# A two-layer diffusion backbone on one core: mixer inputs settled by thirds, the mixer's root on VectorE, the first convolution tap on ScalarE, two score units placed earlier

## The chip, the core and the metric

The kernel runs on one core of one Trainium2 chip. The metric is the device time of one execution in microseconds (us); the time before is the median of three runs. Names used for the engines: PE is the matmul engine (TensorE), DVE is VectorE, ACT is ScalarE, POOL is GpSimd, and SP is SyncE, which issues nearly all transfers.

## What is computed

Two layers of a hybrid backbone over 384 tokens of width 1024: 128 context tokens and 256 latent tokens. Each layer is a half-step feed-forward block, a token mixer, and a second half-step feed-forward block, each behind an RMS norm that is scaled and shifted by a conditioning vector ("ada"). Cut to the mixer:

```python
def _layer(x, cvec, lp, mixer):
    ...
    h = _rmsnorm(x, lp["norm_g"][1]) * (1.0 + sc2) + sh2
    y, ctx = mixer(h)
    x = x + g2 * y
    ...

def _mixer_latent(h, lp, na_kc, na_vc, gq_kc, gq_vc):
    u_hy, na_q, na_k, na_v, gq_q, gq_k, gq_v = _project(h, lp)   # one input projection, q and k RMS-normed
    y_hy = _hyena(u_hy, lp)                                      # short 3-tap convolution, then a long one by FFT
    y_na = _neighbourhood_attention(na_q, na_k, na_v, na_kc, na_vc, lp["na_rpb"])
    y_gq = _window_attention(_axial_rope(gq_q), _axial_rope(gq_k), gq_v, gq_kc, gq_vc, lp["gqa_sink"])
    return _merge(y_hy, y_na, y_gq, lp), ()                      # one output projection

def _short_conv(u, w, b):
    n = u.shape[1]
    up = jnp.pad(u, ((0, 0), (1, 1), (0, 0)))
    return up[:, 0:n] * w[0] + up[:, 1:n + 1] * w[1] + up[:, 2:n + 2] * w[2] + b
```

The long convolution's filter is itself the output of a small sine network, taken to the frequency domain. The context tokens go through the same mixer with dense attention; their keys and values are outputs too (`o_nk`, `o_nv`, `o_gk`, `o_gv`).

## The kernel before

All products with the large weights are done in fp32 as three passes: a weight block comes in as `raw` by a transfer from SP, ACT rounds it to `whi` (L141), DVE subtracts to get `wlo` (L142), the activations are split the same way into `mh` and `ml`, and `mm3` (L303 to L305) issues the three matmuls, 0.18 us apart. A generator of blocks (`get`, `ahead`) keeps the split three blocks ahead of PE. Besides, a slow job runs on DVE through the whole program: the conditioning products (`ada_tick`, L205), a set number of halves of a block for each weight block.

Nothing reorders the instructions: each engine takes them in the order in which the Python code emits them, and waits at the first that isn't ready. The order of the mixer is written out by hand. The main sequence is: the Hyena projection (`hy`, two groups of three output tiles, four weight blocks each), then the projections `pq`, `pk`, `pkv`, `pg`, `vN` (three PSUM tiles `pj` each; PE rows of all of them read `pj<-whi` and so on), then the attention "slots", then the output projection `po`. Between weight blocks `work(budget)` takes steps of the background generators in a list (`bg`): `conv_bg` (the short convolution), `filt` (the filter network, its taps, and its transform `kf`, which ACT copies to `K`), `na_post`, `gk_post`, `gq_post` (norm, scale and rotation of what a projection gave), and `fft`. Each `yield` gives the step's weight against the budget, so one yield less moves everything behind it in the list earlier.

The mixer's own norm is deferred: the projection runs on the unnormed `x` times the ada scale, and the factor is applied to the result. `stats1` (L338) sums the squares by PE (`pss`) and works 1/sqrt by DVE and, from the third operation on, POOL (`rsqrt`, L307: two operations, then 13 that depend on one another). `spread_r` (L345) puts the three values of each token on the diagonals of `dg`, `stats2` (L351) spreads them over the partitions by one product (`pr`) into `R`. `explicit` multiplies the inputs by `R` and ada's scale and shift for the later projections, `settle` splits them into `mh` and `ml`, and `deferred` (L359) applies `R` to a finished tile of the Hyena projection (`hyt`). `HYS = (1, 0)` says after which blocks this happens: the root behind the second block of the first group, `R` behind the first of the second group.

An attention unit is a head pair and a query tile, `hs[0]` to `hs[11]`. A `slot` (L973) does, for successive units, the scores on PE (`sc`), the largest value on DVE (`nm`), the division of an earlier unit's weights (`pr`, L874), their transposition on PE (`pp`), the products with the values (`py`), and the exponentials on ACT (`pr`, L914 and L920). `un_bias` asks for a unit's masks (`nab`). Before, all slots stand behind `vN`.

Buffers matter here. PSUM tiles come from four buffers for each of two tags, "a" and "b"; `kf`, `sc`, `gk`, `pp` and the small products all share "b". Most SBUF tiles of the mixer (`tt`) come from one pool of tag "t", handed out in turn, so that a new tile takes the oldest buffer and waits for everything that still reads it. In the rows of the trace, `pr` names several tiles: the product of `stats2` (L354), and the softmax weights, which the code calls `pr0` and, for the context keys of a unit's first query tile, `pr2`.

`gk_post` ends with the output copies `o_gk` and `o_gv`, issued by POOL (L1053, L1054). POOL's queue holds in this order: the root for gq's norm (13 operations), then `o_gk`, `o_gv`, then `o_nv`.

Of the kernel before, what the change touches and what calls it, by code (L numbers as in the profile page):

```python
# [11 lines left out]
AF = mybir.ActivationFunctionType  # L12
ALU = mybir.AluOpType
# [3 lines left out]
KD = D // P  # L17
# [14 lines left out]
MIXRATE = ((0.75, 0, 0, 0), (0.45, 0, 0, 0))  # L32
# [3 lines left out]
GA = 2  # L36
DLATE = 8
WLATE = False
HYS = (1, 0)
STAT = ((0, 2), (2, 4))  # L40
HPLAN = ({4: (0, 1), 5: (2, 3), 6: (4, 5), 7: (6, 7)}, {4: (0, 1), 5: (2, 3), 6: (4, 5), 7: (6, 7)})
LATE0 = 1
# [36 lines left out]
def _build(ctx, tc, nc, A):  # L79
# [10 lines left out]
    V, S, T = nc.vector, nc.scalar, nc.tensor  # L90

    def tt(name, dt=F32, w=388):
        return tp.tile([P, w], dt, tag="t", name=name)

    def ps(name, tag="b"):
        return psp.tile([P, 512], F32, tag=tag, name=name)

    def sm(name, w=64, dt=F32):
        t = smp.tile([P, 64], dt, tag="s", name=name)
        return t[:, :w]  # L100
# [23 lines left out]
    def small(name, i, n=1):  # L124
        o = SM[name][0] + i
        return sml[:, o:o + n]
# [13 lines left out]
    def split(src, hi, lo):  # L140
        S.activation(hi, src, AF.Copy)  # L141
        V.tensor_tensor(lo, src, hi.bitcast(F32), op=ALU.subtract)  # L142
# [86 lines left out]
    def ada_next():  # L229
        if not adaq:  # L230
            return
        (l, p, j), w = adaq[0]
        ada_half(l, p, j, side_v[0], w)
        side_v[0] ^= 1
        if side_v[0] == 0:
            done.add((l, p, j))
            if p % 3 == 1:
                ada_scale(l, p // 3, j, j + 1)
            adaq.pop(0)
            ada_load()  # L240
# [8 lines left out]
    def ada_tick(rate):  # L249
        credit[0] += 2 * rate  # L250
        while credit[0] >= 1.0:
            credit[0] -= 1.0
            ada_next()
# [84 lines left out]
    def stats1(G=nc.gpsimd):  # L338
        acc = accq
        pss = ps("pss")  # L340
        for t in range(3):
            T.matmul(pss[:, t:t + 1], acc[:, t * P:(t + 1) * P], ones[:, 0:1], start=True, stop=True)
        return rsqrt(pss[:, 0:3], 3, 1.0 / D, G)

    def spread_r(r):  # L345
        dg = tt("dg", w=NT)
        for t in range(3):
            V.tensor_scalar(dg[:, t * P:(t + 1) * P], ident, r[:, t:t + 1], None, op0=ALU.mult)
        return dg

    def stats2(r, dg=None):  # L351
        dg = spread_r(r) if dg is None else dg
        pr = ps("pr")
        T.matmul(pr[:, :NT], ones, dg, start=True, stop=True)  # L354
        R = tt("R", w=NT)
        S.activation(R, pr[:, :NT], AF.Copy)
        return R

    def deferred(pss, R, name):  # L359
        b = sm("bc", 2)  # L360
        V.tensor_copy(b, pss[:, NT:386])
        t = tt(name, w=NT)
        V.tensor_tensor(t, pss[:, :NT], R, op=ALU.mult)  # L363
        return t, b

    def explicit(l, i, R, ks):
        hs = [tt("h", w=NT) for _ in ks]
        for h, k in zip(hs, ks):
            V.tensor_tensor(h, xT[k], R, op=ALU.mult)
        for h, k in zip(hs, ks):  # L370
            for v, a, b in SEG:
                g, sh = gsc[l][:, i, k, v:v + 1], mod[l][:, 3 * i, k, v:v + 1]
                if k in HDVE:
                    V.tensor_scalar(h[:, a:b], h[:, a:b], g, sh, op0=ALU.mult, op1=ALU.add)
                else:
                    S.activation(h[:, a:b], h[:, a:b], AF.Identity, scale=g, bias=sh)
        return list(zip(hs, ks))

    def settle(hk):
        for h, k in hk:  # L380
            split(h, mh[k][:, :NT], ml[k][:, :NT])
# [155 lines left out]
    def mixer(l, after):  # L537
# [11 lines left out]
        def drain(g):  # L549
            while g in bg:  # L550
                try:
                    next(g)
                except StopIteration:
                    bg.remove(g)
# [91 lines left out]
        uc, tm = {}, {}  # L646

        def conv(n):
            up = tt("up")
            for c in (0, 129, 386):  # L650
                V.memset(up[:, c:c + 1], 0.0)
            for v, a, e in SEG:
                S.activation(
                    up[:, 1 + v + a:1 + v + e], tm[n][0][:, a:e], AF.Identity, bias=tm[n][1][:, v:v + 1]
                )
            o = tt(f"uc{n}")
            w3 = [small("conv_w", (l * 3 + q) * 6 + n) for q in range(3)]
            V.tensor_scalar(o[:, 1:386], up[:, 0:385], w3[0], small("conv_b", l * 6 + n), op0=ALU.mult, op1=ALU.add)
            for q in (1, 2):
                V.scalar_tensor_tensor(o[:, 1:386], up[:, q:q + 385], w3[q], o[:, 1:386], op0=ALU.mult, op1=ALU.add)  # L660
            uc[n] = o

        pu = {}
        hk = []
        for grp in range(2):
            for i in range(3):
                pu[grp * 3 + i] = ps(f"hy{i}", "ab"[grp])
            for kb in range(4):
                hi, lo = get()
                for kk, i in order2(2, 3, kb == 3):  # L670
                    k = kb * 2 + kk
                    s = slice(kk * 384 + i * P, kk * 384 + (i + 1) * P)
                    mm3(pu[grp * 3 + i][:, :386], (hi[:, s], lo[:, s]), (mh[k], ml[k]), k == 0, k == KD - 1)
                ahead()
                if (grp, kb) == (0, HYS[0]):
                    rs = stats1()
                if (grp, kb) == (0, 3):
                    dg = spread_r(rs)
                ada_tick(MIXRATE[l][grp])
                if (grp, kb) == (1, HYS[1]):  # L680
                    R = stats2(rs, dg)
                if grp == 1 and kb > HYS[1]:
                    n = KD // (3 - HYS[1]) if HYS[1] != 0 else 3
                    c = kb - HYS[1] - 1
                    hn = explicit(l, 1, R, range(n * c, min(n * c + n, KD)))
                    settle(hk)
                    hk = hn
                    tm[c] = deferred(pu[c], R, "hyt")

        Y = [[None, None] for _ in range(KD)]  # L690

# [2 lines left out]
            split(src, *Y[t])  # L694

        def conv_bg():
            settle(hk)
            yield 1.0
            for n in [n for n in range(6) if n not in tm]:
                tm[n] = deferred(pu[n], R, "hyt")  # L700
                yield 0.55
            for n in range(6):
                conv(n)
                yield 1.2
            for c in range(2):
                V.tensor_tensor(uc[c][:, 1:386], uc[c][:, 1:386], uc[2 + c][:, 1:386], op=ALU.mult)
            yield 0.95

        def project(n, kper, mid):
            pt = [ps(f"pj{t}", "a") for t in range(3)]  # L710
            for kb in range(KD // kper):
                hi, lo = get()
                for kk, t in order2(kper, 3, kb == KD // kper - 1):
                    k = kb * kper + kk
                    s = slice(kk * n, (kk + 1) * n)
                    c = slice(t * P, (t + 1) * P)
                    mm3(pt[t][:, :n], (mh[k][:, c], ml[k][:, c]), (hi[:, s], lo[:, s]), k == 0, k == KD - 1)
                ahead()
                ada_tick(MIXRATE[l][2])
                if kb < KD // kper - 1:  # L720
                    mid(kb)
            out = []
            for t in range(3):
                o = tt("pj", w=NT)
                S.activation(o[:, :n], pt[t][:, :n], AF.Copy)
                out.append(o)
            mid(KD // kper - 1)
            return out
# [108 lines left out]
        def whole(kb):  # L837
            work(BUD[0])
# [8 lines left out]
        q_it = add(na_post(pq, False), True)  # L847
        loads2()
        pk = project(384, 2, whole)
        k_it = add(na_post(pk, True), True)  # L850
# [122 lines left out]
        def slot():  # L973
            s = slot_n[0]
            slot_n[0] += 1
            if s == 0:
                un_bias(hs[0])
                un_bias(hs[1])
            if s + 2 < len(hs):
                un_bias(hs[s + 2])  # L980
            if s < len(hs):
                un_score(hs[s])
            if 0 <= s - 1 < len(hs):
                un_norm(hs[s - 1])
            if 0 <= s - 2 < len(hs):
                un_turn(hs[s - 2])
            if 0 <= s - 3 < len(hs) and hs[s - 3].qi:
                un_pv(hs[s - 3])
            if s < len(hs):
                un_exp(hs[s])  # L990
            work(BUD[2])
# [70 lines left out]
        gk_it = add(gk_post(pkv), True)  # L1062
        pg = project(384, 2, whole)
        gq_it = add(gq_post(pg))
        vN = project(384, 2, whole)
        nc.gpsimd.dma_start(out=A["o_nv"][l], in_=vN[0])
        drain(q_it)
        drain(k_it)
        drain(conv_it)
        drain(filt_it)  # L1070
        fft_it = add(fft())
# [303 lines left out]
```

## Time and profile before

| | us |
|---|---|
| median of three runs | 1540.18 (1538.29 to 1541.30) |
| the profiled execution | 1536.43 |
| its span, first to last instruction | 1534.6 |
| PE busy | 1499.8 (98%) |
| DVE busy | 1144.1 (75%) |
| ACT busy | 649.9 (42%) |
| POOL busy | 70.8 (5%) |

The two mixers lie at about 313 to 478 us and 1062 to 1228 us of the span. A row of a timeline gives start, duration, engine, line and operation; what stands in brackets is the time for which that engine had been idle, and the instruction whose end released it. Matmul durations overlap, so the distance of two starts tells the pace.

### The profile page before, as it was taken

The numbers are of one execution on the slowest core, as the hardware profiler recorded it, in microseconds if no ns is written. First come the engines' busy times: TensorE is split into PE (matmuls) and PEld (weight loads), VectorE is DVE, ScalarE is ACT, GpSimd is POOL, SyncE is SP. The second block draws the span as 40 slices with busy tenths as digits, with TensorE's granted clock in tenths as the row PEclk, the third lists the DMA queues.
The fourth block names the chain that finished last, engine by engine and source line by source line (L and its number), as shares of the span: only waits on it lengthen the run. The fifth ranks groups of instructions, "written<-read, shape, count | busy, mean of one in ns | idle before, by whom it ended". The sixth has DMA issues, their size and how long they took to land. (4 is left out here: it accounts for less than half of the span.)

```text
span 1534.6 us, 23110 instructions
## 1 busy us (share of the span) xinstructions
PE 1499.8 (98%) x8636; PEld 1440.9 (94%) x8636; DVE 1144.1 (75%) x2198; ACT 649.9 (42%) x1191; POOL 70.8 (5%) x181
## 2 busy tenths in 40 slices
PE   6999999999989999999999999999999999999999
PEld 4999999999769999999999999999996799999998
DVE  4489998879787689877858888887897767644444
ACT  3533333346566443333334333333556645433221
POOL 0000000013300000000000000001131000000000
PEclk9999999999999999999999999999999999999999
DMA  9656666564412446655544565556543133344342
GB/s 318 236 183 232 238 226 237 209 195 150 128 42 80 154 162 222 220 196 199 181 152 144 195 238 204 208 210 219 165 124 101 34 124 127 118 158 136 121 153 73
DMA packets 89733, 261.27 MB, mean 170 GB/s; under 512 B 10097, under 2 KB 27796, under 8 KB 89492
## 3 DMA queue, kind: packets, MB, share of 16 engines
q1 hardware_dynamic: 89236, 258.74, 49.2%
q8 instruction: 68, 1.11, 0.3%
q0 software_dynamic: 384, 1.05, 0.2%
q14 instruction: 45, 0.37, 0.1%
HBM read 257.13 MB, written 2.62 MB: 169 GB/s over the span
## 5 line engine op out<-in xcount | busy, mean ns | idle before, releaser
L142 DVE TENSOR_TENSOR wlo<-raw,whi 128x1024 fp32r<-128x1024 f32 (+2 forms) x352 | 394.7, 1125 | 132.3 <-ACT whi L141 131.9
L303 PE MATMUL up<-mh,whi 128*128 128x384 f32 (+1 forms) x1408 | 478.9, 340 | 4.5 <-ACT mh L141 4.2
L305 PE MATMUL up<-mh,wlo 128*128 128x384 f32 (+1 forms) x1408 | 476.9, 339 | 1.3 <-DVE wlo L142 1.2
L304 PE MATMUL up<-ml,whi 128*128 128x384 f32 (+1 forms) x1408 | 477.3, 339 | 0.7 <-DVE ml L142 0.7
L141 ACT ACTIVATE whi<-raw 128x1024 fp32r<-128x1024 f32 (+2 forms) x352 | 339.0, 974 | 270.6 <-PE dn L304 119.5
L205 DVE CUSTOM_DVE_ANT_0 junk<-adaw,cb,sml 128x1024 bf16<-128x1024 f32 x256 | 332.5, 1299 | 2.1
L303 PEld LDWEIGHTS up<-mh,whi 128*128 128x128 f32 x1408 | 265.5, 189 | 7.5 <-ACT mh L141 5.9
L305 PEld LDWEIGHTS up<-mh,wlo 128*128 128x128 f32 x1408 | 265.8, 189 | 2.6 <-DVE wlo L142 2.6
L304 PEld LDWEIGHTS up<-ml,whi 128*128 128x128 f32 x1408 | 265.4, 188 | 2.4 <-DVE ml L142 2.0
L305 PE MATMUL dn<-gh,wlo 128*128 128x384 f32 x704 | 237.2, 337 | 0.0
L304 PE MATMUL dn<-gl,whi 128*128 128x384 f32 x704 | 237.1, 337 | 0.0
L303 PE MATMUL dn<-gh,whi 128*128 128x384 f32 x704 | 236.9, 336 | 0.0
L141 ACT ACTIVATE gh<-t 128x384 fp32r<-128x384 f32 x76 | 39.9, 525 | 294.6 <-DVE t L486 286.4
L303 PEld LDWEIGHTS dn<-gh,whi 128*128 128x128 f32 x704 | 132.2, 188 | 0.0
L304 PEld LDWEIGHTS dn<-gl,whi 128*128 128x128 f32 x704 | 132.1, 188 | 0.0
L305 PEld LDWEIGHTS dn<-gh,wlo 128*128 128x128 f32 x704 | 132.1, 188 | 0.0
L303 PE MATMUL pj<-whi,mh 128*128 128x384 f32 (+1 forms) x240 | 80.1, 334 | 0.8 <-DVE hyt L363 0.8
L305 PE MATMUL pj<-whi,ml 128*128 128x384 f32 (+1 forms) x240 | 78.2, 326 | 0.0
L304 PE MATMUL pj<-wlo,mh 128*128 128x384 f32 (+1 forms) x240 | 78.2, 326 | 0.0
L486 DVE TENSOR_TENSOR t<-up,t 128x384 f32<-128x384 f32 x72 | 39.8, 553 | 50.3 <-PE up L305 50.2
L142 DVE TENSOR_TENSOR gl<-t,gh 128x384 fp32r<-128x384 f32 x76 | 42.4, 558 | 45.0 <-ACT gh L141 45.0
L313 POOL TENSOR_SCALAR rs_r<-rs_r 128x18 int32<-128x18 int32 (+2 forms) x13 | 8.3, 640 | 1172.0 <-DVE rs_r L312 1149.3
(221 smaller groups left out, 1573.2 us busy)
## 6 DMA issues: line engine op xcount, KB each, us to landing
raw<-w SPq DMA_DIRECT2D x184, 512.0 KB, 4.4
adaw<-ada SPq DMA_DIRECT2D x128, 512.0 KB, 3.5
raw<-w SPq DMA_DIRECT2D x64, 448.0 KB, 4.7
raw<-win SPq DMA_DIRECT2D x48, 384.0 KB, 4.0
raw<-w13a SPq DMA_DIRECT2D x32, 384.0 KB, 3.2
adw<-ada SPq DMA_DIRECT2D x32, 192.0 KB, 4.5
raw<-woa SPq DMA_DIRECT2D x16, 384.0 KB, 3.1
nab<-nab SPq DMA_DIRECT2D x24, 192.0 KB, 2.4
```

What stands on the lines that cost most here:

```text
L141: S.activation(hi, src, AF.Copy)
L142: V.tensor_tensor(lo, src, hi.bitcast(F32), op=ALU.subtract)
L205: V.tensor_tensor_reduce(out=junk, in0=w, in1=cb[:, v, :], scale=scale, scalar=small("ada_b", (l * NADA + p) * KD + j), op0=ALU.mult, op1= ...
L303: T.matmul(out, ah, bh, start=start, stop=False)
L304: T.matmul(out, ah, bl, start=False, stop=False)
L305: T.matmul(out, al, bh, start=False, stop=stop)
L313: G.tensor_scalar(r.bitcast(I32), r.bitcast(I32), -1.0, float(0x5F3759DF), op0=ALU.mult, op1=ALU.add)
L486: V.tensor_tensor(t1, PQ[1][:, :NT], t1, op=ALU.mult)
```

## The change

It has three parts. (A) In the Hyena projection the root is worked wholly by DVE behind the second block and spread on `dg` at once; `R` comes behind the third block, and the inputs are scaled by thirds (three, three, two of the eight) behind blocks four to six, settled, with one `hyt` each, behind blocks six to eight. `HYS` goes, the `ada_tick` of the projection takes the first group's rate for three blocks, and `conv_bg` begins without a settle of its own, one `yield` less. (B) The first of the three convolution taps, with the bias, is an activation on ACT instead of a `tensor_scalar` on DVE. (C) Slots 0 and 1 are run inside the `vN` projection, behind its second and third weight block; the background steps of q and k are drained ahead of the first of them. The number of slots doesn't change, so what was in slot 2 comes first behind `vN`.

```diff
--- before.py
+++ after.py
@@ -36,7 +36,6 @@
 GA = 2
 DLATE = 8
 WLATE = False
-HYS = (1, 0)
 STAT = ((0, 2), (2, 4))
 HPLAN = ({4: (0, 1), 5: (2, 3), 6: (4, 5), 7: (6, 7)}, {4: (0, 1), 5: (2, 3), 6: (4, 5), 7: (6, 7)})
 LATE0 = 1
@@ -655,7 +654,9 @@
                 )
             o = tt(f"uc{n}")
             w3 = [small("conv_w", (l * 3 + q) * 6 + n) for q in range(3)]
-            V.tensor_scalar(o[:, 1:386], up[:, 0:385], w3[0], small("conv_b", l * 6 + n), op0=ALU.mult, op1=ALU.add)
+            S.activation(
+                o[:, 1:386], up[:, 0:385], AF.Identity, scale=w3[0], bias=small("conv_b", l * 6 + n)
+            )
             for q in (1, 2):
                 V.scalar_tensor_tensor(o[:, 1:386], up[:, q:q + 385], w3[q], o[:, 1:386], op0=ALU.mult, op1=ALU.add)
             uc[n] = o
@@ -672,20 +673,18 @@
                     s = slice(kk * 384 + i * P, kk * 384 + (i + 1) * P)
                     mm3(pu[grp * 3 + i][:, :386], (hi[:, s], lo[:, s]), (mh[k], ml[k]), k == 0, k == KD - 1)
                 ahead()
-                if (grp, kb) == (0, HYS[0]):
-                    rs = stats1()
-                if (grp, kb) == (0, 3):
-                    dg = spread_r(rs)
-                ada_tick(MIXRATE[l][grp])
-                if (grp, kb) == (1, HYS[1]):
-                    R = stats2(rs, dg)
-                if grp == 1 and kb > HYS[1]:
-                    n = KD // (3 - HYS[1]) if HYS[1] != 0 else 3
-                    c = kb - HYS[1] - 1
-                    hn = explicit(l, 1, R, range(n * c, min(n * c + n, KD)))
-                    settle(hk)
-                    hk = hn
-                    tm[c] = deferred(pu[c], R, "hyt")
+                s = grp * 4 + kb
+                if s == 1:
+                    dg = spread_r(stats1(V))
+                elif s == 2:
+                    R = stats2(None, dg)
+                if s < 3:
+                    ada_tick(MIXRATE[l][0])
+                elif s < 6:
+                    hk += explicit(l, 1, R, range(3 * (s - 3), min(3 * (s - 2), KD)))
+                if s > 4:
+                    settle(hk[3 * (s - 5):3 * (s - 4)])
+                    tm[s - 5] = deferred(pu[s - 5], R, "hyt")
 
         Y = [[None, None] for _ in range(KD)]
 
@@ -694,8 +693,6 @@
             split(src, *Y[t])
 
         def conv_bg():
-            settle(hk)
-            yield 1.0
             for n in [n for n in range(6) if n not in tm]:
                 tm[n] = deferred(pu[n], R, "hyt")
                 yield 0.55
@@ -1062,10 +1059,17 @@
         gk_it = add(gk_post(pkv), True)
         pg = project(384, 2, whole)
         gq_it = add(gq_post(pg))
-        vN = project(384, 2, whole)
+
+        def first_units(kb):
+            whole(kb)
+            if kb == 1:
+                drain(q_it)
+                drain(k_it)
+            if kb in (1, 2):
+                slot()
+
+        vN = project(384, 2, first_units)
         nc.gpsimd.dma_start(out=A["o_nv"][l], in_=vN[0])
-        drain(q_it)
-        drain(k_it)
         drain(conv_it)
         drain(filt_it)
         fft_it = add(fft())
```

How the instructions move is shown at two places. In the program's line numbers of the change, lines are one to three lower than in the kernel before. `[waits X]` says on which engine's or transfer queue's count the instruction waits.

On ACT, in the first layer, from the squares of gq's norm (`q`) on; before:

```order
L738 ACTIVATE q_4028<-pj 128x384 [waits PE_49,Activation_49]
L738 ACTIVATE q_4031<-pj 128x384 [waits DVE_49,Activation_49]
L738 ACTIVATE q_4034<-pj 128x384 [waits DVE_49,Activation_49]
L141 ACTIVATE whi<-raw 128x768 [waits DMAHW0_49,PE_49]
L623 ACTIVATE K_3296<-kf,sml 128x256 [waits DMASW0_49,PE_49]
L623 ACTIVATE K_3299<-kf,sml 128x256 [waits DVE_49,PE_49]
L623 ACTIVATE K_3302<-kf,sml 1x256 [waits DVE_49,PE_49]
L141 ACTIVATE whi<-raw 128x768 [waits DMAHW1_49]
L1057 ACTIVATE kTG_3608<-gk 128x128 [waits PE_49]
L1058 ACTIVATE kTG<-gk 128x256
L623 ACTIVATE K_3297<-kf,sml 128x256 [waits PE_49]
```

and with the change:

```order
L622 ACTIVATE K_3299<-kf,sml 128x256 [waits DVE_49,PE_49]
L622 ACTIVATE K_3302<-kf,sml 128x256 [waits DVE_49,PE_49]
L622 ACTIVATE K_3305<-kf,sml 1x256 [waits DVE_49,PE_49]
L735 ACTIVATE q_4038<-pj 128x384 [waits Activation_49]
L735 ACTIVATE q_4041<-pj 128x384 [waits Activation_49]
L735 ACTIVATE q_4044<-pj 128x384 [waits Activation_49]
L140 ACTIVATE whi<-raw 128x768 [waits DMAHW0_49]
L622 ACTIVATE K_3300<-kf,sml 128x256 [waits DMASW0_49,PE_49]
L622 ACTIVATE K_3303<-kf,sml 128x256 [waits PE_49]
L622 ACTIVATE K_3306<-kf,sml 1x256 [waits DVE_49,PE_49]
L911 ACT_TABLE_LOAD [waits DMASW1_49,DVE_49]
L911 ACTIVATE pr_4124,nm<-sc_4117,nm 128x128 [waits PE_49]
```

The three copies `K` of the filter's first transform stood behind the squares and stand ahead of them now; the copies of the second transform are followed at once by the table load for the first exponential (in the change's last row here), which now waits for a transfer of POOL's queue, `o_gk`, out of the tile whose buffer the exponential's `pr2` takes.

On PE, in the first layer, in the `vN` projection where the transform's matrices (`dft`) meet the taps' sums and differences (`ts`, `td`); before:

```order
L754 MATMUL gk<-ident,pj 128x128 [waits DVE_49]
L754 MATMUL gk<-ident,ra 128x128
L754 MATMUL gk<-ident,ra 128x128 [waits DVE_49]
L622 MATMUL kf<-ts,dft_2938 128x256 [waits Activation_49]
L622 MATMUL kf<-ts,dft_2939 128x256 [waits DMAHW2_49]
L622 MATMUL kf<-td,dft_2940 128x256 [waits DMAHW3_49,Activation_49]
L622 MATMUL kf<-td,dft_2941 128x256 [waits DMAHW4_49]
L622 MATMUL kf<-ts,dft_2940 1x256 [waits Activation_49]
L622 MATMUL kf<-ts,dft_2941 1x256
```

and with the change:

```order
L883 MATMUL sc_4117<-kTN_3423,qTN_3694 128x384 [waits DMAHW5_49,Activation_49]
L883 MATMUL sc_4118<-kTN_3423,qTN_3694 128x384 [waits Activation_49]
L886 MATMUL sc_4117<-kTN_3429,qTN_3694 128x128
L886 MATMUL sc_4118<-kTN_3429,qTN_3694 128x128
L751 MATMUL gk<-ident,pj 128x128 [waits Activation_49]
L751 MATMUL gk<-ident,ra 128x128 [waits DVE_49] x2
L621 MATMUL kf<-ts,dft_2938 128x256 [waits Activation_49]
L621 MATMUL kf<-ts,dft_2939 128x256
L621 MATMUL kf<-td,dft_2940 128x256 [waits Activation_49]
L621 MATMUL kf<-td,dft_2941 128x256
```

The scores `sc` of unit 0 stand right behind the second transform, still inside `vN`. Behind them come the transposes `gk`, then the third transform's `kf`, whose second pair takes the PSUM buffer of `sc` and so waits for the exponential on ACT, and then the third weight block of `vN`.

## Rows read from the trace of the kernel before

**Rows 1.** The page, busy time of the engines: us, share of the span, instructions.

```profile
PE 1499.8 (98%) x8636; PEld 1440.9 (94%) x8636; DVE 1144.1 (75%) x2198; ACT 649.9 (42%) x1191; POOL 70.8 (5%) x181
```

**Rows 2.** The list of PE's waits over the whole span: engine, line, tile, what it waited for, us in total, times, longest us.

```profile
PE pp L935 <- DVE pr L874: 9.0, 7, 1.9
...
PE sc L886 <- ACT PT L940: 1.7, 2, 0.8
...
PE pj L303 <- DVE hyt L363: 0.8, 2, 0.4
...
PE gt L754 <- ACT pr L914: 0.4, 1, 0.4
```

**Rows 3.** PE's timeline in the first mixer, from the last projection's first block on: start us, duration us, engine, line, operation, out<-in, form, count, and in brackets the idle time before it and what ended it.

```profile
394.73 0.45 PE L303 MATMUL pj<-whi,mh 128*128 128x384 f32 x1
...
401.17 0.59 PE L622 MATMUL kf<-ts,dft 128*128 128x256 f32 x2
...
405.90 0.27 PE L754 MATMUL gk<-ident,pj 128*128 128x128 f32 x1
...
406.22 1.03 PE L622 MATMUL kf<-ts,dft 128*128 128x256 f32 x4
...
408.05 1.02 PE L622 MATMUL kf<-ts,dft 128*1 128x256 f32 x4
...
414.08 0.92 PE L886 MATMUL sc<-kTN,qTN 64*128 64x384 f32 x4
...
419.84 0.55 PE L935 MATMUL pp<-ident,pr 128*128 128x128 f32 x3 [1.47 <-DVE pr L874]
...
443.25 0.85 PE L935 MATMUL pp<-ident,pr 128*128 128x128 f32 x6 [1.27 <-DVE pr L874]
```

**Rows 4.** POOL's timeline in the first mixer: the mixer's root, then that of gq and the copy issued behind it, columns as in rows 3.

```profile
321.12 1.21 POOL L313 TENSOR_SCALAR rs_r<-rs_r 128x3 int32<-128x3 int32 x1 [320.67 <-DVE rs_r L312]
...
328.68 0.20 POOL L318 TENSOR_TENSOR rs_r<-rs_r,rs_t 128x3 f32<-128x3 f32 x1
...
401.95 0.76 POOL L313 TENSOR_SCALAR rs_r<-rs_r 128x18 int32<-128x18 int32 x1 [7.97 <-DVE rs_r L312]
...
404.01 0.23 POOL L318 TENSOR_TENSOR rs_r<-rs_r,rs_t 128x18 f32<-128x18 f32 x1
404.31 0.22 POOL L315 TENSOR_TENSOR rs_t<-rs_r 128x18 f32<-128x18 f32 x1
...
407.44 0.59 POOL L1053 DMA_DIRECT2D o_gk<-pj  x1
```

**Rows 5.** PE's timeline, first mixer, from the projection's second block on and at the start of the next projection, columns as in rows 3.

```profile
320.22 0.42 PE L303 MATMUL hy<-mh,whi 128*128 128x386 f32 x1
...
323.33 0.34 PE L305 MATMUL hy<-mh,wlo 128*128 128x386 f32 x1
...
341.09 0.34 PE L305 MATMUL pj<-whi,ml 128*128 128x384 f32 x1
341.82 0.41 PE L303 MATMUL pj<-whi,mh 128*128 128x384 f32 x1 [0.39 <-DVE hyt L363]
```

**Rows 6.** DVE's timeline at the program's start (where the root is worked by DVE) and in the first mixer, columns as in rows 3.

```profile
11.90 0.16 DVE L311 TENSOR_SCALAR rs_a<-pss 128x3 f32<-128x3 f32 x1 [1.53 <-PE pss L342]
...
14.88 0.68 DVE L348 TENSOR_SCALAR dg<-ident,rs_r 128x128 f32<-128x128 f32 x3
...
319.80 0.96 DVE L142 TENSOR_TENSOR wlo<-raw,whi 128x768 fp32r<-128x768 f32 x1
320.67 0.15 DVE L311 TENSOR_SCALAR rs_a<-pss 128x3 f32<-128x3 f32 x1
```

**Rows 7.** The line view of L658, the first tap: engine, operation, count: least, median and largest ns, first and last start, form.

```profile
L658 DVE TENSOR_SCALAR uc<-up,sml x12: 479/482/483, 361.2 to 1136.5; 128x385 f32<-128x385 f32 x12
```

**Rows 8.** ACT's timeline in the first mixer, columns as in rows 3.

```profile
401.80 0.91 ACT L623 ACTIVATE K<-kf,sml 128x256 f32<-128x256 f32 x2 [2.74 <-PE kf L622]
403.32 0.47 ACT L623 ACTIVATE K<-kf,sml 1x256 f32<-1x256 f32 x1 [0.62 <-DVE K L628]
...
409.25 0.47 ACT L623 ACTIVATE K<-kf,sml 1x256 f32<-1x256 f32 x1 [0.62 <-DVE K L637]
...
414.74 1.28 ACT L914 ACT_TABLE_LOAD   x1
416.05 0.37 ACT L914 ACTIVATE pr<-sc,nm 128x128 f32<-128x128 f32 x1
```

**Rows 9.** DVE's timeline in the first mixer, columns as in rows 3.

```profile
399.88 1.46 DVE L739 TENSOR_REDUCE ss<-q 128x6 f32<-128x384 f32 x3
401.38 0.18 DVE L311 TENSOR_SCALAR rs_a<-ss 128x18 f32<-128x18 f32 x1
...
423.27 0.75 DVE L874 TENSOR_SCALAR pr<-pr,nm 128x384 f32<-128x384 f32 x2
```

**Rows 10.** The tile view of `o_gk`, two issues, one a layer: least, median and largest time from issue to landing.

```profile
DMA to landing us min/median/max: 3.6/4.0/4.4
```

**Rows 11.** The list of DMA issues, the copy `o_nk`: queue, count, KB each, median us from issue to landing.

```profile
o_nk<-kg POOLq DMA_DIRECT2D x2, 192.0 KB, 2.5
```

**Rows 12.** Stretches of the span in both mixers (first layer 0, last layer 1): us, then for each engine its busy time and instructions, the granted clock of PE as a share of the full one, the DMA engines' share, GB/s.

```profile
414.00:421.00 7.00, 5.53 (x35) 3.36 (x34) 5.66 (x20) 6.07 (x18) 0.00 (x0) 1.00 0.25 83
...
1169.90:1176.70 6.80, 5.80 (x19) 3.36 (x18) 6.53 (x24) 5.22 (x17) 0.00 (x0) 0.50 0.35 106
```

## The prediction

> **What bounds the kernel now.** I read the shares of the engines first: the matmul engine PE is busy for 98% of the span [rows 1], so only its idle stretches can be won or lost. The list of its waits gives them [rows 2]. Apart from the start of the program they lie in the two mixers, where PE's weighty waits are those of the transposes `pp` for the softmax weights `pr` that DVE scales (9.0 us in seven), then `sc` for ACT's copies (1.7), `pj` for `hyt` (0.8) and `gt` (0.4). The timeline of PE places them: in layer 0 `pp` waits 1.47 us before 419.84 and 1.27 before 443.25 [rows 3]; the longest of the list, 1.9, stands between the two. All that the change can remove is some 6 us a layer; what it can add is not bounded by that. Chances below count as "no change" what lies within 0.2% (3.1 us), about what a measurement of this kernel can tell.
>
> **Root by VectorE, thirds one block earlier.** Now POOL works the root from 321.12 to 328.88 [rows 4], and `pr` (the product that spreads it) comes so late that nobody waits. Afterwards `pr` stands behind the projection's third block. PE reaches that point at 320.22 + 18 matmuls, 323.51 [rows 5]. DVE takes 15 operations and the `dg`: at the program's start the same chain takes 14.88 - 11.90 = 2.98 us, and `dg` 0.68 [rows 6]. From `rs_a` at 320.67 that is 324.33. So PE gets a **new wait of about 0.8 us**. Its bounds are 0.3, if the 15 cost no more than the 0.16 to 0.17 us of their own rows, and 1.7, if the weight split of 0.96 us that DVE does just ahead of them comes late by its own length. In return the inputs are settled a block earlier and the wait for `hyt` goes: 341.82 instead of 341.27 [rows 5], 0.55 us. Net +0.25 us in layer 0, and about +0.1 in layer 1, where the wait that goes is the like: **+0.35**. The ada step that leaves each projection goes where DVE has idle time; I cost it at nothing.
>
> **First tap on ScalarE.** Six times a layer a 0.48 us operation of DVE [rows 7] becomes an activation of the same width, on an engine that is idle over half the span. Neither is waited for: nothing won or lost. If ACT were tight there, the bound is 6 x 0.5 us a layer, but no wait of PE in the conv's stretch names it.
>
> **Two scores moved up.** The matmuls of `hs0` and `hs1` now stand inside the `vN` projection; PE has no less to do. The filter's steps run one slice earlier, because `conv_bg` lost a yield. The order of instructions then shows a **chain that wasn't there**.
>
> (1) On ACT the three copies K of the filter's first transform now stand ahead of the three squares `q` of gq. K waits for `kf`, which PE does behind the first `vN` block: 394.73 + 3.2 = 397.95. K's last copy now ends 2.62 us after `kf` begins (401.17 to 403.79) [rows 3, 8], so 400.57 then. Three squares and DVE's sums behind them take some 1.9 us, the two steps on DVE about 0.6 [rows 9]: POOL begins gq's root at about 403.1; before, 401.95.
>
> (2) POOL needs 5.49 us for it (401.95 to 407.44) [rows 4], and issues the output copy `o_gk` only then, at 408.6. Its landing takes 3.6 to 4.4 us [rows 10]; with the middle, 4.0, it is there at 412.6.
>
> (3) The first exponential writes `pr2` into the buffer from which `o_gk` reads, so ACT stops ahead of its table load until then. ACT would be there at 406.2 (`kf` of the second transform at 402.65, its last copy 3.5 us later, as from 406.22 to 409.72 [rows 3, 8]). Load and exponential take 1.68 us [rows 8]: 414.3.
>
> (4) PE's `kf` pair of the third transform takes the PSUM buffer of that score, so it waits for the exponential, and `vN`'s last two blocks stand behind it. PE gets there at 397.95 + 1.45 (`kf`) + 3.2 (block) + 2.85 (`kf`) + 1.0 (`sc`) + 0.3 (`gk`) + 0.9 (`kf`, first pair) = 407.6 [rows 3]. **PE stands still for 6.7 us in each layer**, inside a dense projection. Bounds: with all of POOL's operations at their 0.30 us pitch (404.01 to 404.31) the root takes 3.9, and landing as for `o_nk` 2.5 [rows 11], which leaves 3.6; with POOL at the 7.76 of [rows 4] and 4.4 for landing it is 9.3.
>
> For the landing I take the row of the same copy. The Trainium skill's "DMA: Bandwidth & Descriptors", section "Anatomy of one DMA — SWDGE (gpsimd) path", fits a POOL-issued copy as 2.0 us plus its bytes over 436e3 per us, an estimate of 2.15 us for these 64 KB; the trace disagrees with its 3.6 to 4.4, and by the page the sum would be 3.7 us lower.
>
> (5) Given back behind it: `pp` of `hs0` is ready, so 1.47 goes; `pp` of `hs1` is not, since DVE's next weight split waits for ACT, whose split stands behind the exponentials. DVE goes on at about 417.7. Up to `hs1`'s scaled weights, which were done at 424.02 [rows 9], I count 9.6 us of its operations still to do then (those from 408.7 on, without idle time and without what it does ahead of the stop): 427.3, a wait of 2.55 (PE is there at 424.8) in place of 1.9. The 1.27 shrinks to about 0.5, `gt`'s 0.4 and `sc`'s 0.84 go, the latter filled by a `cv` that now comes later, and about 0.7 of the `pp` wait behind it is filled so. In all 1.47 - 0.65 + 0.77 + 0.4 + 0.84 + 0.7 = 3.5 of 6.7: **+3.2 us a layer, +6.4**.
>
> (6) The clock. In layer 1 the granted clock now falls to half in 1169.90:1176.70, right behind the first of that mixer's `pp` waits; in layer 0 it stays at 1.00 around the same wait, 1.47 us before 419.84 [rows 3, 12]. That fall costs 0.5 us now, since the waits for DVE swallow the rest, and it goes. A stop of 6.7 us is far longer than either, so I expect the lower level behind it in both layers. Nearly all of a block of 3.2 us would take double: 3.3 more, of which `hs1`'s wait of 2.55 swallows most. Bounds 0 (no fall) and 3.3; I take 1.1, nearer to the swallowed case: **+2.2 - 0.5**.
>
> Sum: 0.35 + 6.4 + 2.2 - 0.5 = **+8.5 us**. On the profiled execution (1536.43 us, span 1534.6) that gives 1544.9; this execution is 3.75 us below the median of the runs shown, 1540.18, so on the median's scale **1548.7 us**.
>
> **Rivals.**
> (a) The stop comes, the clock doesn't fall: 0.35 + 6.4 - 0.5 = +6.3, **1546.5**. For it speaks layer 0's undisturbed wait; against it the length of the new one. The Trainium skill's "TensorE: Matmul & The Clock Gate", section "What's actually happening", says that the engine's default is the throttled level and that an idle stretch brings it back to 1.2 GHz. The trace agrees for layer 1's 1.47 us and does not for layer 0's; by the page the fall comes in both layers.
> (b) **Faster**: the chain doesn't bind. If `o_gk` has landed when ACT comes to its table load at about 406.2, PE waits 0.2 to 1.2 us and the later waits shrink all the same: 3.5 less 0.8 a layer, -5.4 + 0.35, **1535**. It decides at one point, whether the landing comes by 406.2 or at 412.6. Against it: POOL's root alone takes 5.5 us [rows 4] and stands ahead of `o_gk`. For it: in the order before, the same copy landed ahead of the exponential.
> (c) The stop is at its short end, 3.6 us: the waits behind it give back nearly all, 0.1 to 0.6 a layer stays: **1541**, no change.
> (d) The stop is at its long end, 9.3 us, with the fall: 2.6 more a layer, **1554**.
> (e) The change does not do what it says: the scores' matmuls come early, their exponentials don't, and `pp` of `hs0` waits too. That is the forecast without the 1.47: +2.9 in all, 1551.6.
>
> **How the numbers follow.** Forecast 0.45 (own range 1544 to 1555), (a) 0.17, (b) 0.14, (c) 0.13, (d) 0.06, (e) 0.05. The forecast, (a), (d) and (e) are slower, but for 0.03 of them that ends within 3.1 us: 0.70. No change is (c) and that 0.03: 0.16. Faster is (b): 0.14. The range from 1535 to 1556 takes in (b)'s middle and all but the upper edge of (d).
>
> **What would show it.** In the trace after: one idle stretch of PE of 4 to 9 us ahead of `kf` within `vN` in both layers, released by an exponential; ACT's table load at about 412 to 413 with the landing of `o_gk` just before it; POOL's root for gq beginning later than 401.95; the granted clock at half behind it; a wait of `pr` for `dg` of 0.3 to 1.7 us, and none for `hyt`. The prediction is wrong if PE's `vN` blocks run on without that stretch, if the table load comes at 406, or if PE's waits in the mixers fall below what they are now.

## The result, and the profile after

The changed kernel takes **1561.99 us** (median of 4 runs, 1560.10 to 1562.96), against 1539.33 for the kernel before (1538.29 to 1541.30): a ratio of 1.0143, interval 1.0131 to 1.0155. Slower, as forecast, but by 22.7 us instead of 8.5 and outside the range. Its profiled execution took 1562.71 us, its span 1560.9.

Where PE matmuls of the same place begin in the two traces:

| place | before | after | lag |
|---|---|---|---|
| first `dn` of the program | 220.90 | 224.34 | +3.44 |
| mixer 0, first `hy` | 313.27 | 316.71 | +3.44 |
| mixer 0, first `pj` | 340.21 | 344.62 | +4.41 |
| mixer 0, `vN`'s first block | 394.73 | 409.42 | +14.69 |
| behind mixer 0, first `up` | 500.96 | 519.01 | +18.05 |
| mixer 1, first `hy` | 1062.33 | 1078.82 | +16.49 |
| mixer 1, first `pj` | 1089.25 | 1106.45 | +17.20 |
| mixer 1, `vN`'s first block | 1143.77 | 1167.52 | +23.75 |
| behind mixer 1, first `up` | 1250.41 | 1276.97 | +26.56 |

The first 3.4 us lie where the two programs are the same. In the first 50 us the granted clock is at half for 10.2 us after and for 6.8 before, and PE waits 1.4 us longer for its split inputs there; this differs from execution to execution, and the median of before stands 2.9 us above its profiled execution. The rest is made in the mixers, and most of it **between the first `pj` and `vN`**: 10.3 us in layer 0 and 6.6 in layer 1, where the prediction had a gain. From `vN` to `up` it is 3.4 and 2.8.

PE's waits after, over the whole span; they answer to [rows 2]:

```profile
PE kf L621 <- ACT pr L911: 9.1, 2, 4.6
PE pj L302 <- ACT pj L722: 6.5, 2, 3.3
PE pp L932 <- DVE pr L871: 6.2, 6, 1.6
...
PE pj L302 <- DVE hyt L362: 3.4, 3, 2.0
PE cv L819 <- ACT PT L937: 1.7, 2, 0.8
PE pr L353 <- DVE dg L347: 1.2, 2, 0.7
...
PE sc L883 <- ACT qTG L1024: 0.9, 2, 0.4
```

`kf` is the stop that was forecast. `pj` behind ACT's copies out of PSUM, 6.5 us in two, is new and was not. The waits for `hyt`, 0.8 us before, are 3.4. `pp` fell from 9.0 to 6.2. The wait for `PT`, before at `sc`, is as long as it was and stands at `cv` now.

PE's timeline at the four places, first layer (compare [rows 5] and [rows 3]):

```profile
345.82 0.41 PE L302 MATMUL pj<-whi,mh 128*128 128x384 f32 x1 [0.51 <-DVE hyt L362]
...
348.63 0.54 PE L302 MATMUL pj<-whi,mh 128*128 128x384 f32 x1 [2.04 <-DVE hyt L362]
...
376.55 0.28 PE L304 MATMUL pj<-whi,ml 128*128 128x256 f32 x1
380.08 0.58 PE L302 MATMUL pj<-whi,mh 128*128 128x256 f32 x1 [3.24 <-ACT pj L722]
...
421.56 1.03 PE L621 MATMUL kf<-ts,dft 128*128 128x256 f32 x4
427.17 1.16 PE L621 MATMUL kf<-td,dft 128*128 128x256 f32 x2 [4.58 <-ACT pr L911]
```

Each of the long ones stops a dense projection, and a stretch at half clock (0.50, that is 1.2 GHz) begins within the stop or right behind it. Stretches of the span: us, busy time and instructions of PE, PEld, DVE, ACT, POOL, granted clock, DMA share, GB/s (compare [rows 12]):

```profile
348.76:352.17 3.41, 3.41 (x12) 3.41 (x12) 3.41 (x8) 0.00 (x0) 0.00 (x0) 0.50 0.53 153
379.48:386.31 6.83, 6.23 (x29) 6.24 (x30) 5.46 (x17) 5.08 (x12) 0.03 (x1) 0.50 0.70 186
427.26:430.67 3.41, 3.41 (x10) 3.06 (x11) 0.09 (x1) 3.29 (x11) 0.00 (x0) 0.50 0.00 0
```

**The forecast chain is there as read.** POOL's and ACT's timelines after (compare [rows 4, 8, 10]), then the time of `o_gk` from issue to landing:

```profile
417.66 0.87 POOL L312 TENSOR_SCALAR rs_r<-rs_r 128x18 int32<-128x18 int32 x1 [10.26 <-DVE rs_r L311]
...
422.46 0.59 POOL L1050 DMA_DIRECT2D o_gk<-pj  x1
```
```profile
420.36 0.46 ACT L622 ACTIVATE K<-kf,sml 1x256 f32<-1x256 f32 x1 [0.62 <-DVE K L636]
425.37 1.28 ACT L911 ACT_TABLE_LOAD   x1 [4.54 <-DMA o_gk<-pj]
426.66 0.37 ACT L911 ACTIVATE pr<-sc,nm 128x128 f32<-128x128 f32 x1
```
```profile
DMA to landing us min/median/max: 2.8/2.8/2.8
```

ACT is idle for 4.54 us until `o_gk` lands, then loads the table, and the exponential lets PE's `kf` go. The stop is 4.58 us instead of 6.7: POOL's root took 4.8 us (5.49 before) and the copy 2.8 (4.0).

**The one not forecast** lies in the projection of `pkv`. POOL with the root of k's norm, DVE and ACT after, then DVE's same scaling in the second layer:

```profile
369.05 1.12 POOL L312 TENSOR_SCALAR rs_r<-rs_r 128x18 int32<-128x18 int32 x1 [368.61 <-DVE rs_r L311]
...
375.11 1.44 POOL L317 TENSOR_TENSOR rs_r<-rs_r,rs_t 128x18 f32<-128x18 f32 x1
```
```profile
372.43 0.38 DVE L523 TENSOR_SCALAR kq<-arg 64x384 f32<-64x384 f32 x1
372.84 0.35 DVE L524 TENSOR_SCALAR kq<-kq 64x384 f32<-64x384 f32 x1
373.23 1.72 DVE L529 SCALAR_TENSOR_TENSOR arg<-kq,arg 64x384 f32<-64x384 f32 x3
374.98 0.35 DVE L530 TENSOR_SCALAR arg<-arg 64x384 f32<-64x384 f32 x1
375.26 1.21 DVE L141 TENSOR_TENSOR wlo<-raw,whi 128x1024 fp32r<-128x1024 f32 x1
376.59 1.50 DVE L743 TENSOR_TENSOR pj<-pj,rs_r 128x384 f32<-128x384 f32 x3
378.03 0.08 DVE L650 MEMSET up<- 128x1 f32 x3
```
```profile
372.06 0.79 ACT L652 ACTIVATE up<-hyt,bc 128x128 f32<-128x128 f32 x2
378.21 0.71 ACT L657 ACTIVATE uc<-up,sml 128x385 f32<-128x385 f32 x1 [5.37 <-DVE up L650]
378.82 0.83 ACT L140 ACTIVATE whi<-raw 128x768 fp32r<-128x768 f32 x1
379.56 1.23 ACT L722 ACTIVATE pj<-pj 128x384 f32<-128x384 f32 x3
```
```profile
1134.97 1.50 DVE L743 TENSOR_TENSOR pj<-pj,rs_r 128x384 f32<-128x384 f32 x3 [0.42 <-POOL rs_r L317]
```

The border fills of `up` (three memsets, 378.03) stand in DVE's order behind 5.6 us of other work: four steps of the filter's sine (`kq`, `arg`), a weight split (`wlo`) and the scaling of `pj`. ACT's tap reads `up` with border columns, so it waits for the fills: idle for 5.37 us. The scaling needs POOL's root, but that is not what makes the fills late: the root ends at 376.55, DVE's split ahead of the scaling at 376.47, so the root holds DVE up for 0.1 us at most; in layer 1 it is 0.42. Behind the tap in ACT's order stand the split of the next weight and the copies of `pj` out of PSUM, and for those PE waits until 380.08. Before, fills and tap were neighbours on DVE, and at this place ACT had no fill of DVE's to wait for.

### The profile page after: what moved, and what is told of

Same layout as the page of the kernel before. It is cut to its first block, busy times and chain, and to the rows that moved or that the text cites. A ratio compares the mean times of both kernels' runs of the same rounds, so it can differ in the third digit from the quotient of the medians.

```text
span 1560.9 us, 23092 instructions
## 1 busy us (share of the span) xinstructions
PE 1509.5 (97%) x8636; PEld 1449.7 (93%) x8636; DVE 1142.9 (73%) x2212; ACT 655.9 (42%) x1203; POOL 51.0 (3%) x155
## 4 chain that ended last, share of the span: by engine, by line
PE 83%; DVE 7%; ACT 3%; issue 3%; DMA 2%; POOL 1%; SPq 0%; DVEq 0%; ACTq 0%; POOLq 0%
PE up L304 15%; PE up L303 15%; PE up L302 15%; PE dn L303 8%; PE dn L302 8%; PE dn L304 8%; PE po L302 1%; PE po L304 1%; PE po L303 1%; DVE wlo L141 1%; PE pj L302 1%; DMA adw<-ada 1%; PE pj L303 1%; PE pj L304 1%; PE py L958 1%
## 5 line engine op out<-in xcount | busy, mean ns | idle before, releaser
L302 PE MATMUL pj<-whi,mh 128*128 128x384 f32 (+1 forms) x240 | 85.0, 354 | 9.9 <-ACT pj L722 6.5
L303 PE MATMUL pj<-wlo,mh 128*128 128x384 f32 (+1 forms) x240 | 81.9, 341 | 0.0
L304 PE MATMUL pj<-whi,ml 128*128 128x384 f32 (+1 forms) x240 | 81.5, 339 | 0.0
L302 PEld LDWEIGHTS pj<-whi,mh 128*128 128x128 f32 x240 | 48.8, 203 | 17.7 <-issue 10.6
```

The costliest lines, as they stand in the source:

```text
L302: T.matmul(out, ah, bh, start=start, stop=False)
L303: T.matmul(out, ah, bl, start=False, stop=False)
L304: T.matmul(out, al, bh, start=False, stop=stop)
```

## The experiments

All times are medians; the kernel before ran beside each group at 1539.4 to 1539.9 us.

**The tap back on DVE.**

```diff
-            S.activation(o[:, 1:386], up[:, 0:385], AF.Identity, scale=w3[0], bias=...)
+            V.tensor_scalar(o[:, 1:386], up[:, 0:385], w3[0], ..., op0=ALU.mult, op1=ALU.add)
```

> The changed kernel with the first tap put back on DVE. Theory 1 (ACT's tap waits for the border fills that DVE does behind POOL's root of k's norm; the weight split and the copies out of PSUM queue behind it): PE's 3.2 us wait for ACT's pj copies goes in both layers, with the half-clock stretch behind it; the lag taken there was 7.8 and 6.0 us, so about 1548 us. Theory 2 (the tap's 0.7 us on ACT is simply too much for ACT): the same here. Theory 3 (the loss is the root and the late hyt on DVE): at most 2 us less, 1560.

1550.28 us, 11.7 less. PE's list of waits has no `pj` behind ACT any more, and `kf` and `hyt` stand as they were:

```profile
PE kf L621 <- ACT pr L909: 9.1, 2, 4.6
...
PE pp L930 <- DVE pr L869: 6.2, 6, 1.6
PE pj L302 <- DVE hyt L362: 3.4, 3, 2.0
```

**The tap on ACT, the borders one step earlier.** `up` of the next step is taken and its borders filled at the start of each step. The cut leaves out `frame` itself and `frame(0)` ahead of the loop.

```diff
         def conv(n):
-            up = tt("up")
-            for c in (0, 129, 386):
-                V.memset(up[:, c:c + 1], 0.0)
+            if n < 5:
+                frame(n + 1)      # takes ups[n + 1] and fills its borders
+            up = ups.pop(n)
```

> The changed kernel, tap on ACT, but each tile's borders are filled by DVE one convolution step earlier. Theory 1: ACT has nothing of DVE to wait for at the tap, so nearly all of what the first run wins is won here too: about 1549 us, and the 5.4 us idle stretch of ACT ahead of a tap is gone. Theory 2: ACT does as much as before, so 1560 to 1562.

1550.98 us, 11.0 less: nearly the same win with ACT doing as much as in the changed kernel. ACT's timeline at that place:

```profile
371.06 0.79 ACT L659 ACTIVATE up<-hyt,bc 128x128 f32<-128x128 f32 x2
371.88 0.71 ACT L664 ACTIVATE uc<-up,sml 128x385 f32<-128x385 f32 x1
373.21 0.85 ACT L140 ACTIVATE whi<-raw 128x768 fp32r<-128x768 f32 x1 [0.62 <-PE pj L304]
374.27 0.49 ACT L730 ACTIVATE pj<-pj 128x384 f32<-128x384 f32 x1 [0.20 <-PE pj L304]
```

The tap follows its `up` at once, and what ACT waits for behind it is PE. So it is the fills coming late, not ACT's load. The tap takes 0.71 us there, on DVE 0.48 [rows 7].

**Each part alone on the kernel before.** The tap, its lines of the change's diff and no others:

> The kernel before with only the tap moved to ACT. Theory 1: ACT waits for DVE's fills in the projections of the mixer here as well; 6 to 7 us a layer, 1551 to 1553 us. If the fills come in time in the old order of the background steps, 1540. Theory 2: 2 to 4 us, 1543.

1547.85 us, +8.3, less than the first theory had. The wait is there without the other parts, 2.3 us in each layer, and a half-clock stretch of 3.41 us behind both (a third, at 1220.41, has only stops of 0.9 us and less near it):

```profile
PE pj L303 <- ACT pj L727: 4.6, 2, 2.3
```

The root by DVE and the thirds, that is the hunks on `HYS`, on the loop over the projection's blocks and on `conv_bg`:

> The kernel before with only the root by DVE and the inputs by thirds. My prediction's sum had +0.35 us for it, 1540. The trace of the changed kernel speaks for more: 0.8 and 0.6 us at the product that spreads the root, 2.4 and 0.4 us at the projection that waits for hyt (now behind three splits), and a half-clock stretch of 3.4 us in layer 0: 1543 to 1546.

1544.14 us, +4.6 (ratio 1.0030, 1.0016 to 1.0043). Its waits are those of the changed kernel:

```profile
PE pj L302 <- DVE hyt L362: 3.4, 3, 2.0
...
PE pr L353 <- DVE dg L347: 1.2, 2, 0.7
```

The two slots, the last hunk:

> The kernel before with only the two score units moved into the vN projection. The background steps keep their old slices here, so pr2 takes another buffer and its exponential does not wait for the copy o_gk. Theory 1 (PE's stop in vN is the landing of o_gk): the stop is 0.2 to 1.5 us, the first pp wait goes, 1534 to 1538 us. Theory 2 (PE stops because the third transform takes the score's PSUM buffer, whatever ACT waits for): a stop of 3 us or more a layer, 1543 to 1547.

1536.56 us, 2.9 less, a ratio of 0.9981 (0.9972 to 0.9990): **a little faster**, clear of the scatter, though within the 3.1 us that the prediction counted as no change. In kind this is rival (b), at about half of its gain. ACT waits only for DVE's maximum, then loads the table, and PE stops for 1.34 us:

```profile
406.56 0.47 ACT L623 ACTIVATE K<-kf,sml 1x256 f32<-1x256 f32 x1 [0.62 <-DVE K L628]
407.89 1.28 ACT L914 ACT_TABLE_LOAD   x1 [0.87 <-DVE nm L902]
```
```profile
407.33 1.03 PE L622 MATMUL kf<-ts,dft 128*128 128x256 f32 x4
409.70 0.48 PE L622 MATMUL kf<-td,dft 128*128 128x256 f32 x1 [1.34 <-ACT pr L914]
```

The three parts alone add up to +9.9 us; together they cost 22.7. The difference has to come from the parts meeting. One candidate is the `yield` that `conv_bg` lost, which belongs to the second of these parts.

**The lost yield put back.**

```diff
         def conv_bg():
+            yield 1.0
             for n in [n for n in range(6) if n not in tm]:
```

> The changed kernel with the lost yield put back at the start of the convolution's background steps, and nothing else. The filter then runs one slice later, pr2 takes another buffer, and no exponential waits for o_gk. Theory: PE's stop in vN is 1.3 us instead of 4.6, as with the copy by SP, and the wait behind the tap is like that of the tap alone (2.3 us instead of 3.2): 1550 to 1556. Rival (the lost yield has nothing to do with it): 1560 to 1562.

1549.33 us, 12.7 less, which is just the sum of the parts alone. `kf` waits 2.7 us in two instead of 9.1, `pj` for ACT 4.6 instead of 6.5, and the mixers hold 10.2 us at half clock instead of 23.9. One yield moves the filter by a slice, and with it the turn of the buffers: without it `pr2` takes the one that `o_gk` still reads. With it the first exponential begins at 419.17, before `o_gk` is issued (419.87).

**`o_gk` issued by SP** in the changed kernel.

```diff
-            nc.gpsimd.dma_start(out=A["o_gk"][l], in_=pts[0][:, :P])
+            nc.sync.dma_start(out=A["o_gk"][l], in_=pts[0][:, :P])
```

> The changed kernel with o_gk issued by SP, so that it doesn't stand behind POOL's root. Theory 1: the table load comes up to 4 us sooner, PE's stop of 4.6 us shrinks below 1.5 and the half-clock stretch behind it goes: 1555 to 1557. Theory 2: the stop stays over 3 us, 1560 to 1562. If SP itself is late at that place (it waits for free raw buffers), something between.

1552.93 us, 9.1 less, though its runs spread from 1545.6 to 1555.2, so that the size is known only to be between about 5 and 14. The exponential waits for DVE's maximum now, and PE's stop there is 1.33 us:

```profile
421.95 1.28 ACT L911 ACT_TABLE_LOAD   x1 [1.29 <-DVE nm L899]
```

The profiled execution is the slowest of the four. In it the half-clock stretch had been expected to go, but it moved: in each layer one of 3.41 us now follows a later stop of 1.83 us for `pp`.

**`hyt` ahead of the splits** in the changed kernel.

```diff
-                    settle(hk[3 * (s - 5):3 * (s - 4)])
                     tm[s - 5] = deferred(pu[s - 5], R, "hyt")
+                    settle(hk[3 * (s - 5):3 * (s - 4)])
```

> The changed kernel with each deferred scaling (hyt) put ahead of the split of its third instead of behind it. Theory: PE's waits for hyt at the start of the next projection (0.5 and 2.0 us in layer 0, 0.9 in layer 1) go, with the half-clock stretch at 349 us: 1557 to 1559. Rival (DVE is short of time there, whatever the order): the splits come later instead and PE waits for ml or mh, 1561 to 1563.

1557.08 us, 4.9 less: one wait of 1.0 us for `hyt` is left of three, and the half-clock stretch at 349 us is gone. The rival did not come.

**All three mended.**

> The changed kernel with all three mends: borders filled one step earlier, o_gk issued by SP, hyt ahead of the splits. If the three causes add up (11 + 6 + 4 us): 1540 to 1543. If one wait takes the place of another: 1546 or more.

1537.57 us, 24.4 less than the change; the three mends alone had 11.0, 9.1 and 4.9, in all 25.0. That is below the 1540 to 1543 expected. Within the scatter the causes add up, and with them gone the change is at 0.9988 (0.9979 to 0.9998) of the kernel before.

**Better than both.** The slots alone leave PE the stop of the table load, so the next run brings the table in early: on the kernel with the two slots alone

```diff
             yield from sin_layer(p2[:HD, :NT], fbm[l][1], small("freq", l * 2 + 1), h2[:HD])
+            S.activation(exd, ones[:, 0:1], AF.Exp)
```

> The two slots alone, as in the fifth run, plus a one-column exponential on ACT behind the filter's second sine, which brings the exponential table in early. Theory: the 1.34 us stop of PE in vN that is left there is the table load of 1.28 us; it goes to 0.1 or less in both layers: 1533.5 to 1535. Rival (the stop is DVE's maxima or the score itself): 1536 to 1537 as in the fifth run.

1532.91 us, ratio 0.9955 (0.9940 to 0.9970). PE's `kf` goes on:

```profile
405.07 1.03 PE L624 MATMUL kf<-ts,dft 128*128 128x256 f32 x4
406.17 1.13 PE L624 MATMUL kf<-td,dft 128*128 128x256 f32 x4
```

With `hyt` ahead of the splits as well, in the loop of the kernel before:

```diff
+                    tm[c] = deferred(pu[c], R, "hyt")
                     settle(hk)
                     hk = hn
-                    tm[c] = deferred(pu[c], R, "hyt")
```

> As the run before, and the deferred scaling hyt ahead of the split of its third, in the old places of the kernel before (root on POOL). Theory: PE's 0.40 us wait for hyt goes in both layers, 0.5 us each: 1532.5 to 1534. Rival: the splits come later and PE waits for them, no gain.

**1532.51 us**, 0.9953 (0.9938 to 0.9968): no wait for `hyt` is left in PE's list, but the 0.4 us less is within the scatter. And with the tap on ACT, its borders filled a step earlier by the edit of the second run:

> As the run before, and the first tap on ACT with its borders filled one step earlier. DVE has 5.8 us less to do in all; PE's waits for DVE's scaled weights (1.63, 0.48, 1.0 us a layer) lie 40 us and more behind the taps, so I expect no gain there: within 1 us of the run before. If ACT's 0.7 us a tap comes in the way of its copies: up to 2 us more.

1533.79 us, 0.9959 (0.9945 to 0.9973): 1.3 us more, within the scatter, so no gain, as expected.

## Why the prediction was wrong, step by step

- **"First tap on ScalarE ... Neither is waited for: nothing won or lost"** is the step that failed, and the largest. It asked whether ACT has room and whether PE waits for ACT there before; it did not ask what the moved operation itself waits for. Its input had a writer on DVE, three small fills, and these stood behind 5.6 us of other work in DVE's order. (The expectation of the first run puts the fills behind POOL's root; the trace has at most 0.1 and 0.4 us of waiting for it.) Measured: 3.2 to 3.3 us of stop in each layer with 6.83 us at half clock, 11 to 12 us in all, 8.3 by itself.
- **"the inputs are settled a block earlier and the wait for `hyt` goes"** failed in its second half. What it left out is DVE's order at the end of the projection, before (first line) and after:

```profile
334.99 0.54 DVE L363 TENSOR_TENSOR hyt<-hy,R 128x384 f32<-128x384 f32 x1
```
```profile
343.65 1.50 DVE L141 TENSOR_TENSOR ml<-h,mh 128x384 fp32r<-128x384 f32 x3 [0.30 <-ACT mh L140]
...
345.13 0.55 DVE L362 TENSOR_TENSOR hyt<-hy,R 128x384 f32<-128x384 f32 x1
...
346.46 1.49 DVE L141 TENSOR_TENSOR ml<-h,mh 128x384 fp32r<-128x384 f32 x3
...
347.94 0.55 DVE L362 TENSOR_TENSOR hyt<-hy,R 128x384 f32<-128x384 f32 x1
```

Before, the first `hyt` had no splits ahead of it and was done 4.7 us before the first `pj` (340.21). Now each `hyt` stands behind the splits of a third, and the first is done 1.1 us after the first `pj` (344.62): in layer 0 the first `hyt` comes 0.5 us after PE wants its buffer and the second 2.0. Instead of -0.55 a layer the lag grew by 2.4 us in layer 0 (4.41 at the first `pj`, 348.63 against 341.82 of [rows 5] at the third tile's) and 0.4 in layer 1; with the clock it was worth 4.9 us. The new wait for `dg`, forecast at 0.8, was 0.7 and 0.4.
- **Two scores moved up** was right in mechanism and place. The stop was sized at 6.7 us and measured 4.6, both POOL's root and the landing being shorter than their rows before. From `vN` to `up` the lag grew by 3.4 and 2.8 us where 4.3 and 3.8 had been forecast. That this came near is in part luck: the stop is 2.1 us shorter, and what step (5) gives back, less what the clock takes, is 1.2 and 1.8 us instead of 2.4 and 2.9. Of the give-back, the 0.84 of `sc` did not come, since the wait for `PT` stands at `cv` now, and the 0.4 of `gt` was counted in each layer where [rows 2] has it once. Taking the wait for `o_gk` away by SP was worth 9.1 us, where forecast and rival (b) lie 13.7 apart. `pp` of `hs0` was ready, so rival (e) is out; that of `hs1` waited 1.6 us, not 2.55. What made the wait bind at all was the lost yield, as the run that put it back shows; step (3) had seen that `pr2` takes the buffer that `o_gk` reads. For the copy's landing the Trainium skill's "DMA: Bandwidth & Descriptors", section "Anatomy of one DMA — SWDGE (gpsimd) path", gives an estimate of 2.15 us; the trace after has 2.8, between that and the 4.0 of [rows 10], and the other traces with the copy on POOL have 1.9 to 4.7.
- **The clock** fell behind that stop in both layers, as step (6) said, so rival (a) is out. The Trainium skill's "TensorE: Matmul & The Clock Gate", section "What's actually happening", has an idle stretch bring the clock back to 1.2 GHz; the stops of 4.58 and 4.56 us agree with it. The clock fell at the stops that I had not seen too, and they cost more than their length: the mixers hold 23.9 us at half clock after and 6.8 before.
- The range missed because it was built around one chain. The other two parts stood in the sum with 0.35 us and nothing, and none of the rivals gave a price for either of them being late; the tap's own bound, 6 x 0.5 us a layer, went into none.

## What to carry to other kernels

When an operation moves to another engine, look up who writes each of its inputs, the small fills too, and where those writers stand in their own engine's order: a writer just ahead on the same engine costs no wait, but from another engine the operation waits for all that stands ahead of that writer there, here 5.6 us of work for three fills of one column. Then ask what stands behind the moved operation on its new engine. A step more or less in a hand-made order also turns a buffer pool, so check which reader each new tile's buffer still has.

## What the runs showed of the hardware

In the mixers the half-clock stretches were 3.41 or 6.83 us long. In all the traces together each of the 24 stops of PE of 2.0 us or more there had one begin within it or at most 1.3 us behind it; of the 41 between 1.3 and 1.9 us, 6 had one begin within 2 us behind them. The same 13 operations of POOL on 18 columns took from 4.8 to 7.5 us (417.66 to 422.46, 369.05 to 376.55), and the copy `o_gk`, issued by POOL, from 1.9 to 4.7 us to land. The table load took 1.28 us (425.37 here), with the exponential right behind it. At the start of the program, which no kernel here changes, the first `dn` began between 220.90 and 225.34 us, so the times of two single executions can differ by some 4 us for that alone.
